# Expert layer of a hybrid transformer: all column groups of the whole float32 passes held together in one order, last piece first

## The chip, the cores and the metric

The kernel runs on one core of a Trainium2 chip. The metric is the device time of one execution in microseconds (us); the lower the better. Times of before are the median of three runs; the profile is of one further execution.

## What is computed

Two layers of a backbone over 256 latent and 256 context tokens of width 1024. Layer 0 ends in a dense SwiGLU, layer 1 in a mixture of eight SwiGLU experts, each token going to the two with the highest logits. The change is in the experts alone:

```python
def swiglu(h, w_gu, w_down):
    g, u = jnp.split(h @ w_gu, 2, axis=-1)
    return (jax.nn.silu(g) * u) @ w_down

def moe_swiglu(h, w_router, w_gu, w_down):
    logits = (h @ w_router).astype(jnp.float32)
    top_v, top_i = lax.top_k(logits, TOP_K)
    gates = jax.nn.softmax(top_v, axis=-1)
    out = jnp.zeros_like(h)
    for e in range(N_EXPERTS):
        w_e = jnp.sum(jnp.where(top_i == e, gates, 0.0), axis=-1).astype(h.dtype)
        out = out + w_e[..., None] * swiglu(h, w_gu[e], w_down[e])
    return out
```

All is float32; an expert has a hidden width of 1408, so its weights are 11.5 MB of gate-and-up and 5.8 MB of down.

## The kernel before

Everything up to the experts (the two mixers and the dense feed-forward) takes the first 840 us or so and is not touched.

The experts are sorted by the number of their tokens. Tokens are gathered into slots, 128 to a pass, and the slots of a pass are the rows of the output in PSUM, one slot to a partition. `PASSES` says which experts a pass holds: four passes have 128 slots of one expert; one has 32 slots of expert 1 and 96 of expert 4; one has 64, 32 and 32 slots of experts 5, 6 and 7. `Piece` (line 233 on) is the part of a pass that belongs to one expert. A pass of one expert is *split*: its weights come from HBM into a raw buffer, ScalarE rounds them to `wh` (line 268), VectorE takes the rest `wl` (line 271), and TensorE does three fast matmuls of 128x512 for each product. There are three pairs of `wh` and `wl`. A pass of several experts is *whole*: its pieces use the raw float32 weights without splitting, and each matmul handles a quarter of 32 slots, that is 32 columns of the TensorE array and 32 partitions of PSUM. A quarter is a **column group**: group 0 writes partitions 0 to 31, group 1 partitions 32 to 63, and so on. `product` (line 1523) issues them; a piece of 64 slots gives two matmuls, of 96 three.

`expert` (line 1474) is one job: 22 blocks of gate-and-up weights per expert (six column tiles `nt`, of two or four blocks `b`; a block holds two steps `kk` of the contraction, in the last `nt` four of half width), then 11 of down weights `f`. `blocks` (line 1503) loads a block of each expert of the job, in the order of the pieces; `products` (line 1532) is called for each `kk` and issues the matmuls of all pieces of a pass:

```python
            for c in pieces:
                self.mgu = product(out, c, get(c), ws[c.expert], s, start, stop)[-1]
```

`moe` (line 1632) runs the four jobs of `JOBS` in turn. The third job has a split pass (expert 1) and the whole pass of experts 1 and 4 (tiles `xgv` and `aTv`). Beside them runs the job called `last`, the whole pass of experts 5, 6 and 7 (tiles `xgw` and `aTw`): it is a generator, advanced at the steps that the table `LAST` names, so that its gate-and-up lies among the other jobs' work, and its down passes (per half `h` of the output) end the program.

Instructions are put in order by a scheduler that simulates the program, engine by engine, from the order of writing and the data they need; `inorder` (line 516) adds a dependence without a semaphore, so that one instruction stands behind another on its engine. Before, the pieces of a whole pass write different partitions and read different weights, and nothing holds their matmuls together.

Loads are issued by SP's queue in a fixed order into a ring of buffers: five of the pool `rawp`, eight of the pool `act`, one or two slots in old activations (`raw`, line 274). A load waits until the last reader of its buffer is done. SP also reads the number of experts with too many tokens (`overi`, line 1850), for the branch at the end.

Of the kernel before, what the change touches and what calls it, by code (L numbers as in the profile page):

```python
# [239 lines left out]
class Kern:  # L240
# [1233 lines left out]
    def expert(self, eids, passes, ys, last=False):  # L1474
# [28 lines left out]
        def blocks(gu, *at):  # L1503
            ws = {}
            for e in eids:
                if gu and self.w0:
                    ws[e] = None, self.w0.pop(0)
                    continue
                nt, b = at
                if gu:  # L1510
                    ap = a["mg0"][self.eid[e], nt, b] if nt < 5 else a["mg1"][self.eid[e], b]
                    n, parts = 1024, 1
                elif last:
                    n = min(2, 11 - nt)
                    ap = a["md"][self.eid[e], nt:nt + n, :, b * 512:b * 512 + 512].rearrange("f p c -> p f c")
                    n, parts = n * 512, n
                else:
                    ap, n, parts = a["md"][self.eid[e], nt], 1024, 1
                r = self.raw(ap, n, parts, split=e not in whole)
                ws[e] = r, self.split(r) if e in split else None  # L1520
            return ws

        def product(out, c, x, w, s, start, stop):
            if c.whole:
                return [self.mm(out[c.row + q:c.row + q + QUART], x[:, 0, q:q + QUART], w[0][:, s], start=start, stop=stop)
                        for q in range(0, c.n, QUART)]
            wh, wl = (t[:, s] for t in w[1])
            return [self.mm(out, x[:, 0], wh, start=start, stop=False),
                    self.mm(out, x[:, 0], wl, start=False, stop=False),
                    self.mm(out, x[:, 1], wh, start=False, stop=stop)]  # L1530

        def products(out, pieces, get, ws, s, start, stop):

            for c in pieces:
                self.mgu = product(out, c, get(c), ws[c.expert], s, start, stop)[-1]

        for nt in range(6):
            hw = 256 if nt < 5 else P
            kb = 2 if nt < 5 else 4
            ps = [self.ps("g", "mgu") for _ in passes]  # L1540
            for b in range(8 // kb):
                ws = blocks(True, nt, b)
                for p, (pieces, _) in zip(ps, passes):
                    for kk in range(kb):
                        k = b * kb + kk
                        products(p[:, :2 * hw], pieces, lambda c: c.x[:, :, k], ws,
                                 slice(kk * 2 * hw, kk * 2 * hw + 2 * hw), k == 0, k == 7)
                if (last or b % 2) and b < 8 // kb - 1:
                    yield
            for p, (pieces, _) in zip(ps, passes):  # L1550
                th = self.tmp("mth")[:, :hw]
                A.activation(th, p[:, :hw], AF.Tanh, scale=0.5)
                V.scalar_tensor_tensor(th, th, 1.0, p[:, :hw], op0=OP.add, op1=OP.mult)
                self.glu = V.scalar_tensor_tensor(th, th, 0.5, p[:, hw:2 * hw], op0=OP.mult, op1=OP.mult)
                trans(pieces, th, nt, hw // P)
            yield
# [10 lines left out]
        if last:  # L1567
            pieces, gate = passes[0]
            ys += [mp.tile([P, 2, 512], F32R, tag="ymoe", name="ylast", bufs=2),
                   mp.tile([P, 512], F32, tag="aT", name="ylast1", bufs=1)]  # L1570
            for h in range(2):
                p = self.ps("g", "mdn")
                for f in range(11):
                    if f % 2 == 0:
                        ws = blocks(False, f, h)
                    products(p, pieces, lambda c: c.a[:, :, f], ws, slice(f % 2 * 512, f % 2 * 512 + 512), f == 0, f == 10)
                    if f % 2:
                        yield
                for q in range(2):
                    s = slice(q * 256, q * 256 + 256)  # L1580
                    y = self.tmp("yg")[:, :256] if h == 0 else ys[1][:, s]
                    self.ylast = V.scalar_tensor_tensor(y, p[:, s], gate(), self.rowg[:, 2 * h + q],
                                                        op0=OP.mult, op1=OP.mult)
                    if h == 0:
                        self.hilo(ys[0], s, y)
                yield
            return
        py = [[self.ps("g", "mdn") for h in range(2)] for _ in passes]
        for f in range(11):
            ws = blocks(False, f, 0)  # L1590
            for pys, (pieces, _) in zip(py, passes):
                for h in range(2):
                    products(pys[h], pieces, lambda c: c.a[:, :, f], ws, slice(h * 512, h * 512 + 512), f == 0, f == 10)
            if f % 2:
                yield
# [292 lines left out]
```

## Time and profile before

| | before |
|---|---|
| median of 3 runs | 1285.9 us (1285.56 to 1288.61) |
| profiled execution | 1285.85 us |
| its span, first to last instruction | 1284.1 us |
| TensorE (PE) busy | 1248.9 us, 97% |
| VectorE (DVE) busy | 693.7 us, 54% |
| ScalarE (ACT) busy | 498.9 us, 39% |
| DMA | 263.12 MB, mean 205 GB/s |

The profile's page gives busy times over the whole span, and then groups of instructions. Further views answer questions about a stretch: busy time by window, the instructions of an engine in order of time, who waited for whom, and the chain of work that ended last. PE is the matmul, PEld the load of its stationary operand, which overlaps. In the views a tile is named as out<-in; `mgu` is a gate-and-up result in PSUM, `mdn` a down result. A matmul's recorded length contains its way through the pipe, so how long it occupies TensorE is read from the start of the next.

### The profile page before, as it was taken

The page shows a single profiled execution, that of the slowest core. Times are in us where ns is not written, and L with a number is a line of the kernel's source. Part 1 is how long each engine was busy: PE and PEld are TensorE (multiplying, and loading weights), DVE is VectorE, ACT ScalarE, POOL GpSimd, SP SyncE. Part 2 cuts the span into 40 slices and gives each one's busy share as a digit, 9 for nine tenths or more (in the row PEclk, how much of TensorE's full clock was granted, in tenths as well). Part 3 has the DMA queues.
Part 4 walks back from the last instruction along what each step waited for, and adds up shares of the span by engine and source line. Part 5 has one row for each costly group of instructions (what it writes and reads, how often), then busy time and mean ns, then how long its engine had stood idle before and what let it go on. Part 6 is the DMA issues. An engine that isn't in the chain of part 4 may idle for free.

```text
span 1284.1 us, 18115 instructions
## 1 busy us (share of the span) xinstructions
PE 1248.9 (97%) x6654; PEld 866.6 (67%) x6654; DVE 693.7 (54%) x1523; ACT 498.9 (39%) x938; POOL 8.9 (1%) x30
## 2 busy tenths in 40 slices
PE   6999999999999999999999999989999999999995
PEld 3777666777878888888868878955656533545632
DVE  4554674356433443443367777677767533446741
ACT  3443543224322322322235445545655323444521
POOL 0000000000000000000000000000000000000000
PEclk9999999999999999999999999999999999999998
DMA  9535343539342223222224553569897887699695
GB/s 379 203 132 197 131 141 122 176 135 390 106 157 89 92 99 99 91 89 99 99 75 141 194 212 130 188 227 372 317 372 289 308 287 295 218 368 353 249 368 208
DMA packets 82849, 263.12 MB, mean 205 GB/s; under 512 B 8128, under 2 KB 16448, under 8 KB 82752
## 3 DMA queue, kind: packets, MB, share of 16 engines
q1 hardware_dynamic: 82176, 259.79, 55.6%
q0 software_dynamic: 576, 2.10, 0.5%
q8 instruction: 54, 0.88, 0.3%
q14 instruction: 43, 0.35, 0.1%
HBM read 260.80 MB, written 1.05 MB: 204 GB/s over the span
## 4 chain that ended last, share of the span: by engine, by line
PE 91%; DMA 4%; DVE 2%; ACT 2%; issue 1%; SPq 0%; ACTq 0%; DVEq 0%
PE g L326 21%; PE mgu L326 18%; PE dps L326 10%; PE gps L326 9%; PE ups L326 9%; PE mdn L326 8%; PE adaps L326 4%; DMA raw<-in_md_dram 3%; PE vps L326 2%; PE attS L326 2%; PE rowbc L326 1%; PE yps L326 1%; PE scat L326 1%; PE gath L326 1%; PE attO L326 1%
## 5 line engine op out<-in xcount | busy, mean ns | idle before, releaser
L271 DVE TENSOR_TENSOR wl<-raw,wh 128x512 fp32r<-128x512 f32 (+1 forms) x354 | 300.6, 878 | 209.9 <-ACT wh L268 208.3
L268 ACT ACTIVATE wh<-raw 128x512 fp32r<-128x512 f32 (+1 forms) x354 | 262.3, 780 | 310.7 <-PE dps L326 80.8
L326 PE MATMUL g<-hmix,wh 128*128 128x512 f32 (+1 forms) x640 | 182.6, 364 | 0.3 <-DVE hmix L537 0.2
L326 PEld LDWEIGHTS g<-hmix,wh 128*128 128x128 f32 x640 | 112.6, 189 | 33.7 <-issue 11.0
L326 PE MATMUL gps<-hffn,wh 128*128 128x512 f32 x320 | 125.6, 395 | 0.0
L326 PE MATMUL ups<-hffn,wh 128*128 128x512 f32 x320 | 125.5, 394 | 0.0
L326 PE MATMUL mgu<-wh,xg 128*128 128x512 f32 (+1 forms) x384 | 120.9, 384 | 1.0 <-ACT wh L268 1.0
L326 PE MATMUL g<-hmix,wl 128*128 128x512 f32 (+1 forms) x320 | 115.5, 361 | 0.0
L326 PE MATMUL dps<-aT,wh 128*128 128x512 f32 x352 | 111.1, 394 | 0.0
L326 PEld LDWEIGHTS mgu<-wh,xg 128*128 128x128 f32 x384 | 70.2, 188 | 30.9 <-ACT wh L268 10.3
L326 PEld LDWEIGHTS dps<-aT,wh 128*128 128x128 f32 x352 | 66.0, 188 | 16.6 <-ACT wh L268 0.8
L326 PE MATMUL mgu<-wl,xg 128*128 128x512 f32 (+1 forms) x192 | 76.5, 398 | 0.4 <-DVE wl L271 0.2
L326 PE MATMUL mgu<-raw,xgw 128*32 128x512 f32 (+1 forms) x376 | 72.0, 564 | 0.3 <-DMA raw<-in_mg_dram 0.3
L326 PEld LDWEIGHTS gps<-hffn,wh 128*128 128x128 f32 x320 | 60.4, 189 | 14.9 <-DVE gth L1120 0.8
L326 PEld LDWEIGHTS ups<-hffn,wh 128*128 128x128 f32 x320 | 60.5, 189 | 14.2
L326 PE MATMUL dps<-aT,wl 128*128 128x512 f32 x176 | 69.6, 396 | 0.0
L326 PEld LDWEIGHTS g<-hmix,wl 128*128 128x128 f32 x320 | 60.4, 189 | 8.4 <-issue 0.9
L326 PE MATMUL ups<-hffn,wl 128*128 128x512 f32 x160 | 63.4, 396 | 0.0
L326 PE MATMUL gps<-hffn,wl 128*128 128x512 f32 x160 | 63.4, 396 | 0.0
L326 PE MATMUL mgu<-raw,xgv 128*32 128x512 f32 (+1 forms) x384 | 61.8, 563 | 0.0
L326 PE MATMUL mdn<-wh,aT 128*128 128x512 f32 x176 | 59.7, 404 | 0.0
L326 PEld LDWEIGHTS mgu<-wl,xg 128*128 128x128 f32 x192 | 36.1, 188 | 33.2 <-DVE wl L271 12.6
(356 smaller groups left out, 1725.7 us busy)
## 6 DMA issues: line engine op xcount, KB each, us to landing
raw<-in_mg_dram SPq DMA_DIRECT2D x162, 512.0 KB, 6.4
raw<-in_ada_dram SPq DMA_DIRECT2D x96, 512.0 KB, 5.0
raw<-in_md_dram SPq DMA_DIRECT2D x79, 512.0 KB, 7.4
raw<-in_fg_dram SPq DMA_DIRECT2D x44, 512.0 KB, 3.5
raw<-in_wi_dram SPq DMA_DIRECT2D x40, 512.0 KB, 4.9
raw<-in_fd_dram SPq DMA_DIRECT2D x22, 512.0 KB, 3.2
raw<-in_wo_dram SPq DMA_DIRECT2D x16, 512.0 KB, 5.0
xres<-in_mg_dram SPq DMA_DIRECT2D x9, 512.0 KB, 6.3
```

The source lines that it names most:

```text
L268: up = self.A.activation(h, src, AF.Copy)
L271: sub = self.V.tensor_tensor(lo, src, h.bitcast(F32), op=OP.subtract)
L326: return self.E.matmul(out, l, r, start=start, stop=stop, skip_group_check=True)
```

## The change

`products` now takes the pieces in reverse, so that the piece whose weights are loaded last goes first, and for a whole pass it holds all matmuls of one call in that order, behind the last matmul of the call before on the same block. A split pass has one piece and is as it was.

```diff
         def products(out, pieces, get, ws, s, start, stop):
 
-            for c in pieces:
-                self.mgu = product(out, c, get(c), ws[c.expert], s, start, stop)[-1]
+
+            ms = [m for c in reversed(pieces) for m in product(out, c, get(c), ws[c.expert], s, start, stop)]
+            if pieces[0].whole:
+                self.inorder(ws.setdefault("turn", [])[-1:] + ms)
+                ws["turn"] = ms
+            self.mgu = ms[-1]
```

What the scheduler makes of it on TensorE, in the second job, where one block of the job `last` lies among the split matmuls of the gate-and-up (`raw,xgw` are whole matmuls, `wh,xg` and `wl,xg` split ones). Before:

```order
3081 L326 MATMUL mgu<-raw,xgw 32x512 x2
3082 L326 MATMUL mgu<-wl,xg 128x512
3083 L326 MATMUL mgu<-wh,xg 128x512 x2
3084 L326 MATMUL mgu<-raw,xgw 32x512
3085 L326 MATMUL mgu<-wl,xg 128x512
3086 L326 MATMUL mgu<-wh,xg 128x512
3087 L326 MATMUL mgu<-raw,xgw 32x512 x5
3088 L326 MATMUL mgu<-wh,xg 128x512
```

Now:

```order
3070 L326 MATMUL mgu<-wl,xg 128x512
3071 L326 MATMUL mgu<-wh,xg 128x512 x2
3072 L326 MATMUL mgu<-raw,xgw 32x512 x8
3073 L326 MATMUL mgu<-wl,xg 128x512
3074 L326 MATMUL mgu<-wh,xg 128x512 x2
```

The eight whole matmuls of the block stand together where the last five stood.

On TensorE in the third job's gate-and-up, `raw,xgv` being the whole pass of experts 1 and 4. Before:

```order
3285 L326 MATMUL mgu<-raw,xgv 32x512
3286 L326 MATMUL mgu<-wh,xg 128x512
3287 L1494 MATMUL atr<-constp,mth 128x128 x2
3288 L326 MATMUL mgu<-raw,xgv 32x512 x7
3289 L326 MATMUL mgu<-wl,xg 128x512
```

Now:

```order
3260 L326 MATMUL mgu<-wh,xg 128x512 x2
3261 L1494 MATMUL atr<-constp,mth 128x128 x2
3262 L326 MATMUL mgu<-raw,xgv 32x512 x8
3263 L326 MATMUL mgu<-wl,xg 128x512
3264 L326 MATMUL mgu<-wh,xg 128x512 x2
```

The one matmul of expert 1 that stood ahead has joined the seven.

On TensorE at the end, where the down passes of `last` begin among those of the fourth job. Before:

```order
3681 L326 MATMUL mdn<-raw,aTw 32x512
3682 L326 MATMUL mdn<-wl,aT 128x512
3683 L326 MATMUL mdn<-wh,aT 128x512 x2
3684 L326 MATMUL mdn<-wl,aT 128x512
3685 L326 MATMUL mdn<-wh,aT 128x512
3686 L326 MATMUL mdn<-raw,aTw 32x512 x5
```

Now:

```order
3630 L326 MATMUL mdn<-raw,aTw 32x512 x8
3631 L326 MATMUL mdn<-wl,aT 128x512
3632 L326 MATMUL mdn<-wh,aT 128x512
3633 L326 MATMUL mdn<-wl,aT 128x512
3634 L326 MATMUL mdn<-wh,aT 128x512
3635 L326 MATMUL scat<-selT,ymoe 128x256 x2
3636 L326 MATMUL mdn<-raw,aTw 32x512 x8
```

Here too a block of 2, 1 and 5 has become one run of 8. The order of loads on SP is the same but for a few neighbours in the first two jobs, and the read of `overi`, which moves ahead of eight loads.

## Rows read from the trace of the kernel before

**Rows 1.** Busy time by stage: window, length, PE, PEld, DVE, ACT, POOL (instructions), PE clock, DMA share, GB/s

```profile
844.00:1004.00 160.00, 157.54 (x764) 98.58 (x763) 114.48 (x289) 90.19 (x188) 0.00 (x0) 1.00 0.90 336
1004.00:1114.00 110.00, 109.71 (x686) 46.26 (x684) 46.70 (x97) 36.12 (x81) 0.00 (x0) 1.00 0.76 276
1114.00:1153.00 39.00, 39.00 (x251) 16.65 (x248) 16.34 (x28) 15.05 (x28) 0.00 (x0) 1.00 0.91 333
1153.00:1223.50 70.50, 70.16 (x388) 43.73 (x387) 52.33 (x103) 39.16 (x79) 0.00 (x0) 1.00 0.82 298
1223.50:1270.00 46.50, 45.06 (x250) 17.17 (x250) 10.30 (x22) 5.70 (x12) 0.00 (x0) 1.00 0.96 355
```

**Rows 2.** Matmuls in order of time, third job: start us, length us, engine, line, tiles, shape, count

```profile
1018.12 0.64 PE L326 MATMUL mgu<-wh,xg 128*128 128x512 f32 x2
1018.59 0.40 PE L326 MATMUL mgu<-wl,xg 128*128 128x512 f32 x1
...
1019.15 1.05 PE L326 MATMUL mgu<-raw,xgv 128*32 128x512 f32 x2
1020.13 0.50 PE L326 MATMUL mgu<-wh,xg 128*128 128x512 f32 x1
...
1026.08 1.06 PE L326 MATMUL mgu<-raw,xgv 128*32 128x512 f32 x8
1027.08 0.50 PE L326 MATMUL mgu<-wl,xg 128*128 128x512 f32 x1
...
1027.73 1.06 PE L326 MATMUL mgu<-raw,xgv 128*32 128x512 f32 x8
```

**Rows 3.** Matmuls in order of time, one block of the job `last` in the second job

```profile
923.97 1.05 PE L326 MATMUL mgu<-raw,xgw 128*32 128x512 f32 x4
...
925.83 1.05 PE L326 MATMUL mgu<-raw,xgw 128*32 128x512 f32 x2
...
927.46 1.91 PE L326 MATMUL mgu<-raw,xgw 128*32 128x512 f32 x10
929.30 0.50 PE L326 MATMUL mgu<-wh,xg 128*128 128x512 f32 x1
```

**Rows 4.** Matmuls in order of time, whole matmuls of half width, third job

```profile
1107.99 1.07 PE L326 MATMUL mgu<-raw,xgv 128*32 128x256 f32 x16
1109.00 0.44 PE L1494 MATMUL atr<-constp,mth 128*128 128x128 f32 x2
```

**Rows 5.** Matmuls in order of time, first block of `last`; in brackets idle time and releaser

```profile
851.66 1.05 PE L326 MATMUL mgu<-raw,xgw 128*32 128x512 f32 x4 [0.35 <-DMA raw<-in_mg_dram]
852.90 1.04 PE L326 MATMUL mgu<-rawo,xgw 128*32 128x512 f32 x2 [0.20 <-DMA rawo<-in_mg_dram]
...
855.84 0.62 PE L326 MATMUL mgu<-rawo,xgw 128*32 128x512 f32 x1 [0.53 <-DMA rawo<-in_mg_dram]
855.85 0.62 PE L326 MATMUL mgu<-raw,xgw 128*32 128x512 f32 x2
```

**Rows 6.** Who waited for whom, 844 to 1284: us in total, times, longest

```profile
PEld mdn L326 <- DMA raw<-in_md_dram: 7.7, 10, 1.2
PEld mgu L326 <- DMA raw<-in_mg_dram: 5.8, 16, 0.8
```

**Rows 7.** Waits of SP's queue, which issues the loads, 844 to 1284

```profile
SPq L307 <- PE mgu L326: 131.1, 70, 7.3
```

**Rows 8.** Busy time by window in the first job, columns as in the first group

```profile
857.60:870.40 12.80, 12.80 (x54) 8.41 (x53) 10.34 (x20) 9.25 (x19) 0.00 (x0) 1.00 1.03 412
...
857.60:902.00 44.40, 44.40 (x221) 28.45 (x221) 34.62 (x105) 26.16 (x55) 0.00 (x0) 1.00 1.00 381
```

**Rows 9.** DMA queues, 1219.3 to 1270: packets, MB, share of 16 engines; then the issues

```profile
q1 hardware_dynamic: 9024, 17.30, 93.5%
...
raw<-in_md_dram SPq DMA_DIRECT2D x30, 512.0 KB, 10.2
raw<-in_md_dram SPq DMA_DIRECT2D x6, 256.0 KB, 9.2
```

**Rows 10.** Chain of work that ended last, 1215 to 1284: start us, us, what

```profile
1219.32 4.16 DMA raw<-in_md_dram
```

**Rows 11.** Instructions of line 1850, the read of the overflow count: count, ns, first and last start us

```profile
L1850 SPq TENSOR_LOAD <-overi x1: 292/292/292, 914.8 to 914.8; - x1
```

## The prediction

> **What bounds the kernel now.** I read busy time by stage first, then the matmuls in order of time, then the waits, for the engines and for the queue that issues the loads. The profiled execution took 1285.85 us (span 1284.1 and 1.75 around it), which is the median of the runs (1285.9), so the sum below is made against 1285.85. The change touches only the experts, from about 844 us on, and I cut that part into five: A, the first two expert jobs (844 to 1004); B, the gate-and-up passes of the third job (1004 to 1114); C, its down passes (1114 to 1153); D, the fourth job (1153 to 1223.5); E, the down passes of the job called "last" (1223.5 to 1270). In A to D TensorE is busy for 376.4 of 379.5 us at a granted clock of 1.00 (the 2.4 GHz level), with VectorE at 42 to 74% and DMA at 0.76 to 0.91 of its time [rows 1]. What TensorE does there is therefore on the path, unless something else is close behind it.
>
> A busy TensorE is not a well-used one, and the order of time shows it. A whole float32 matmul writes 32 of the 128 output partitions, and the trace has two records for each. A run with one such matmul (x2) lasts 0.98 us until the next matmul starts (1019.15 to 1020.13); a run of four on different column groups (x8) lasts 1.00 (1026.08 to 1027.08) [rows 2]. Four cost what one costs. A run of five (x10, from 927.46) lasts 1.84 [rows 3]. I call a **slot** what runs side by side: matmuls that follow each other on different column groups, until a group comes again. From one slot to two the run grows: a slot costs 0.86 us (1.84 less 0.98) however full it is, and half of that at half width (16 records, two half slots, 1.01 us in all) [rows 4].
>
> A run also costs something to enter and leave. From 1026.08 to 1027.73 one slot and two ordinary matmuls take 1.65 us; ordinary ones follow each other at 0.235 (two from 1018.12 to 1018.59) [rows 2]. 1.65 - 0.86 - 0.47 = 0.32 us per run.
>
> **The change, step by step.** It removes and adds no instruction of a kind: same matmuls, same loads. It puts pieces together.
>
> For the "last" job's gate-and-up (pieces of 64, 32 and 32 slots, so column groups 0 and 1, then 2, then 3), a block of two k stands before as runs of 2, 1 and 5: groups 01, then 2, then 3012 and 3, four slots in three runs; after, 8 in one run, two slots. In the trace these are the x4, x2 and x10 records at 923.97, 925.83 and 927.46 [rows 3]. For the third job's mixed pass (pieces of 32 and 96), 1 and 7 become 8: three slots and two runs become two and one. I counted the whole order in this way, before against after:
> - A: 41 slots in 30 runs, now 22 in 11. 19 x 0.86 + 19 x 0.32 = 22.4 us. In the very first block TensorE waited for the third expert's weights anyway, until 855.84 [rows 5]; two slots and a run stood ahead of that moment and their removal only lengthens the wait, 2.0 us. Left: 20.4.
> - B: 65 slots and 8 half ones in 36 runs, now 51 and 9 in 27. 13.5 x 0.86 + 9 x 0.32 = 14.5.
> - C: nothing (22 slots in 12 runs both times: there the two pieces already stood together).
> - D: 13 slots and 11 halves in 16 runs, now 11 and 8 in 9. 3.5 x 0.86 + 7 x 0.32 = 5.2.
> - E: 28 slots in 13 runs, now 22 in 7: 7.1 us of TensorE, which I cost at nothing. What hides it is the loader: 36 loads, 17.30 MB, take 0.94 of all DMA time from the issue of the first to 1270 [rows 9]: they land in an unbroken stream, and TensorE has nothing to do with how fast. If that cover were thin the 7.1 us would come in addition; if the held order keeps a slot back until the third weights are there, up to one slot, 0.9 us, would be lost.
>
> Sum on TensorE ahead of E: 20.4 + 14.5 + 5.2 = 40.1 us.
>
> E begins when its first load is issued, at 1219.32 [rows 10], and that load waits for a buffer that the fourth job's splitting frees. The splitting follows TensorE through its three buffers of split weights, so E moves up with D.
>
> Now what is close behind. **VectorE**: in 857.6 to 902 it is busy 34.62 of 44.40 us [rows 8]. Three blocks of the last job lie in it; each loses two slots and two runs, 2.4 us, so the stretch would shrink to 37.2 and VectorE would stand at 93%, with only three buffers of split weights between it and TensorE. I charge half of the 7.2 us there. **DMA**: loads reach 412 GB/s when the queue is full (857.6 to 870.4) [rows 8]. A moves 336 GB/s x 160 us = 53.8 MB, 130 us at that rate: 30 us of room for 20.4. B and D have 36 and 19 us of room for 14.5 and 5.2. So the loader follows on the whole, though not in each stretch; I charge 1 us. In SP's queue a few loads of A change places with a neighbour, which costs nothing as long as they come early. The read of the overflow count, at 914.8 before [rows 11], now stands ahead of eight loads that it stood behind; SP may wait there for VectorE to make the count, by at most what those eight loads take (8 x 512 KB at 381 GB/s, 11 us) and more likely by a few us, with some fifteen buffers loaded or loading by then. I cost it at nothing, and at 11 us for the range.
>
> The added order: between pieces it makes TensorE wait for the piece whose weights come last. What stands behind it in TensorE's queue is all the ordinary work, and VectorE and ScalarE wait for that. It costs nothing while the third weights are there in time. All waits of TensorE for expert weights from 844 on are 5.8 + 7.7 us [rows 6], while the loader waits 131.1 us for buffers that TensorE has yet to read [rows 7]: loads wait for TensorE, not TensorE for loads. From both sides: nothing as now, or at most two landings of 512 KB at 412 GB/s, 2.5 us, per block if the loads had no lead. I take nothing, since both rows stand on that side.
>
> 40.1 - 3.6 - 1 = 35.5. **Forecast: 1285.85 - 35.5 = 1250 us.**
>
> The row says that four groups cost what one costs. The Trainium skill, "TensorE: Matmul & The Clock Gate", Part 3, Measured speedup, gives less for packing: 2.38 for three column tiles and 3.07 for four row tiles, so that a full group would cost 1.3 of a single matmul. With a pair at the price of one, the slots ahead of E would by that give back some 25 us instead of 29, and the forecast would be some 1254; the trace differs (1.00 against 0.98 us) and I go by it.
>
> **Rivals.**
> 1. The loader or VectorE takes back much of it. For: in 857.6 to 902 DMA already moves 381 GB/s, and D has 0.82 with an idle stretch at its end, so it is fuller before. If the gain is lost wherever these two are near their limit, that is all 7.2 us of 857.6 to 902, about as much for the three blocks of the second job near 950 to 980 where loads come fast, and half of D: 17 us less than 40.1, so 23 us, 1263. Against: the 131 us that the loader stands waiting. Chance 0.18.
> 2. It gets **slower**: the order turns the last weights into a wait. Place: each of the 22 blocks of the "last" job's gate-and-up. Price: before, groups 0 and 1 could start on the first weights; now all wait for the third, two landings or 2.5 us later, 55 us over 22 blocks. It decides where the loads' lead over TensorE is under 2.5 us, as in the first block [rows 5]. If the lead were gone everywhere: 1285.85 + 55 - 40.1 = 1301. Against it stand the two waits [rows 6, 7]. Chance 0.03.
> 3. It does not do what it says: column groups that read different weights do not run side by side, so that the slots stay. Then only the runs count, 34 of them ahead of E x 0.32 = 11 us, 1275. Against: at 855.84 two different weight buffers start within 0.02 us [rows 5]. Chance 0.03.
> 4. Nothing to be seen, within 0.3% (3.9 us, about what a measurement of this kernel can tell): a reshuffle of the order elsewhere (the gather of tokens moves by some matmuls) eats all. The stages run at 99% TensorE, so there is little slack for it to upset. Chance 0.02.
>
> **Numbers.** The forecast has 0.74. Its own range is 1241 (nothing charged for VectorE and DMA, and some of E) to 1257. The range that should hold 8 in 10 reaches into rival 1: 1240 to 1268. Faster by over 0.3%: 0.74 + 0.18 + 0.03 = 0.95. Same: 0.02. Slower: 0.03.
>
> **What would show it.** Right: in the trace after, runs of the last job read x16 and last about 1.85 us, none is x2; A shrinks to some 140 us, B to 96, C stays at 39, D at about 65; E stays near 47 from its first load to its last; TensorE's waits for expert weights stay under some 20 us and DMA rises above 0.95 in A. VectorE in the first job goes above 0.85. Wrong: an x16 run that lasts over 2.1 us (slots are not free), waits for the mg loads of tens of us (rival 2), or stage C longer.

## The result, and the profile after

| | before | after |
|---|---|---|
| median (lowest to highest, 4 runs each, side by side) | 1286.3 us (1285.56 to 1288.61) | **1246.88 us** (1245.71 to 1248.32) |
| profiled execution; span | 1285.85; 1284.1 | 1245.71; 1243.9 |
| TensorE busy | 1248.9 us, 97% | 1198.1 us, 96% |

The ratio of after to before is 0.9691, 95% interval 0.9674 to 0.9709: 39.4 us less, where 1250 us was forecast and 1240 to 1268 given as the range.

The view by stage, with the cuts moved to where the stages now begin (busy time of each engine, granted clock, DMA share, GB/s), answers to [rows 1] in the same columns:

```profile
844.00:984.30 140.30, 136.88 (x771) 98.90 (x770) 115.21 (x292) 90.48 (x188) 0.00 (x0) 0.98 0.99 383
984.30:1081.40 97.10, 97.10 (x690) 45.96 (x689) 47.37 (x99) 36.82 (x83) 0.00 (x0) 1.00 0.86 321
1081.40:1121.40 40.00, 40.00 (x254) 17.49 (x252) 17.93 (x29) 16.32 (x31) 0.00 (x0) 1.00 0.89 334
1121.40:1185.80 64.40, 63.84 (x382) 42.85 (x381) 51.28 (x101) 37.06 (x75) 0.00 (x0) 1.00 0.87 325
1185.80:1230.00 44.20, 33.29 (x242) 13.34 (x243) 8.79 (x20) 5.68 (x12) 0.00 (x0) 1.00 0.95 351
```

A, B, C and D last 140.3, 97.1, 40.0 and 64.4 us; the prediction named 140, 96, 39 and 65. In A DMA has gone to 0.99 of its time. In A the clock is 0.98 and TensorE is idle for 3.4 us: that was not foreseen, and one place holds most of both (below). VectorE in the first job was to go above 0.85 and stands at 0.84.

What the change was to make, a block of the last job in one run, stands in the order of time of TensorE in the first job:

```profile
869.62 0.61 PE L326 MATMUL mgu<-wh,xg 128*128 128x512 f32 x2
870.16 1.93 PE L326 MATMUL mgu<-raw,xgw 128*32 128x512 f32 x16
872.01 0.50 PE L326 MATMUL mgu<-wl,xg 128*128 128x512 f32 x1
```

16 records, that is eight whole matmuls, last 1.85 us until the next starts (870.16 to 872.01). Before, five of them lasted 1.84 and the first three had runs of their own [rows 3]. All blocks of the last job in A and B stand like this. In D the first three are still cut, into 10 and 6, 6 and 10, and 14 and 2 records, so that the sign "none is x2" did not quite come true; the prediction's count of D, 11 slots and 8 halves in 9 runs, has these cuts in it.

The first block of the last job is the exception. In order of time, and then in windows across it:

```profile
853.09 0.40 PE L326 MATMUL mgu<-wl,xg 128*128 128x512 f32 x1
856.54 1.07 PE L326 MATMUL mgu<-rawo,xgw 128*32 128x512 f32 x2 [3.06 <-DMA rawo<-in_mg_dram]
...
857.40 1.06 PE L326 MATMUL mgu<-rawo,xgw 128*32 128x512 f32 x2
...
859.83 0.50 PE L326 MATMUL mgu<-wl,xg 128*128 128x512 f32 x1
```

```profile
849.70:853.10 3.40, 3.40 (x21) 2.91 (x19) 2.62 (x9) 1.90 (x5) 0.00 (x0) 1.00 0.87 306
853.10:856.50 3.40, 0.39 (x2) 0.00 (x0) 2.04 (x10) 0.37 (x1) 0.00 (x0) 0.94 0.95 353
856.50:859.90 3.40, 3.36 (x17) 0.66 (x17) 0.00 (x0) 0.00 (x0) 0.00 (x0) 0.56 1.02 416
859.90:863.30 3.40, 3.40 (x15) 2.81 (x16) 1.99 (x4) 2.65 (x6) 0.00 (x0) 1.00 1.02 414
```

TensorE waits 3.06 us for the third expert's weights, and then works at a granted clock of 0.56: a pass over all four groups takes 0.86 us (856.54 to 857.40) where half of the 0.86 us of a slot is usual, so the clock stands at the lower of its two levels, 1.2 GHz. The block takes 3.29 us instead of 1.85.

For E, the DMA queue from the issue of its first load (1178.7) to 1229.4, and the loads in the chain that ended last. These answer to [rows 9, 10]:

```profile
q1 hardware_dynamic: 9024, 17.30, 93.3%
...
raw<-in_md_dram SPq DMA_DIRECT2D x30, 512.0 KB, 10.7
raw<-in_md_dram SPq DMA_DIRECT2D x6, 256.0 KB, 9.3
```

```profile
1183.53 11.85 DMA raw<-in_md_dram
...
1195.51 9.36 DMA raw<-in_md_dram
...
1204.99 10.02 DMA raw<-in_md_dram
...
1215.12 10.71 DMA raw<-in_md_dram
```

The same 36 loads with the same 17.30 MB, now from 1178.7 on instead of 1219.3, take 0.93 of all DMA time, and the chain that ended last is four loads one behind the other. E has moved up by 40.6 us and is no shorter for it: from the issue of the first load to the landing that the chain waits for last it takes 47.0 us before (1219.32 to 1266.33) and 47.1 now (1178.70 to 1225.83).

The waits of TensorE and its weight loads for expert weights, 844 to the end, against [rows 6]:

```profile
PEld mdn L326 <- DMA raw<-in_md_dram: 16.9, 13, 3.8
PE mdn L326 <- DMA raw<-in_md_dram: 9.8, 10, 2.9
PEld mgu L326 <- DMA rawo<-in_mg_dram: 3.5, 1, 3.5
PE mgu L326 <- DMA rawo<-in_mg_dram: 3.1, 1, 3.1
PEld mgu L326 <- DMA raw<-in_mg_dram: 2.7, 8, 0.4
```

Those for down weights (`md`) have grown. They lie in E, all but 0.7 us of the 16.9, where TensorE is through sooner and waits for the stream. By the weight loads alone the waits for expert weights are 16.9 + 3.5 + 2.7 = 23.1 us, so that the prediction's sign, under some 20 us, failed; it failed in E, where TensorE's time does not count (e2 below). Those for gate-and-up weights (`mg`) are the one wait of the first block and little else. In SP's queue the loader's wait for TensorE has shrunk by about the gain, from 131.1 [rows 7] to 92.0 us, and its wait for the overflow count is 0.6 us:

```profile
SPq L307 <- PE mgu L326: 92.0, 41, 6.3
...
SPq L1854 <- DVE overi L1362: 0.6, 1, 0.6
```

### The profile page after: what moved, and what is told of

Read it like the earlier page. It is cut to its first block, busy times and chain, and to the rows that moved or that the text cites. A ratio compares the mean times of both kernels' runs of the same rounds, so it can differ in the third digit from the quotient of the medians.

```text
span 1243.9 us, 18096 instructions
## 1 busy us (share of the span) xinstructions
PE 1198.1 (96%) x6654; PEld 862.0 (69%) x6654; DVE 692.7 (56%) x1523; ACT 498.6 (40%) x938; POOL 8.9 (1%) x30
## 4 chain that ended last, share of the span: by engine, by line
PE 90%; DMA 5%; DVE 2%; ACT 1%; issue 1%; SPq 1%; ACTq 0%; DVEq 0%
PE g L326 22%; PE mgu L326 17%; PE dps L326 10%; PE gps L326 9%; PE ups L326 9%; PE mdn L326 7%; PE adaps L326 3%; DMA raw<-in_md_dram 3%; PE vps L326 2%; PE attS L326 2%; PE rowbc L326 1%; PE yps L326 1%; PE gath L326 1%; PE attO L326 1%; PE scat L326 1%; PE attT L757 1%
## 5 line engine op out<-in xcount | busy, mean ns | idle before, releaser
L326 PE MATMUL mgu<-wh,xg 128*128 128x512 f32 (+1 forms) x384 | 117.5, 380 | 0.0
L326 PE MATMUL adaps<-raw,s 128*32 128x512 f32 x384 | 56.6, 619 | 0.2 <-DMA raw<-in_ada_dram 0.2
L1099 DVE SCALAR_TENSOR_TENSOR xres<-dps,mods,xres 128x256 f32<-128x256 f32 x64 | 27.6, 478 | 43.3 <-PE dps L326 43.3
```

The source lines that it names most:

```text
L326: return self.E.matmul(out, l, r, start=start, stop=stop, skip_group_check=True)
L1099: self.V.scalar_tensor_tensor(self.x[:, d, s], ps[:, s], gt[:, j:j + 1], self.x[:, d, s], op0=OP.mult, op1=OP.add)
```

## The experiments

In all of them a "unit" is 0.86 us, what one full-width whole matmul occupies its column group for. Stage lengths in the table are of the profiled executions, in us, from the start of TensorE's first matmul of each stage; the last column is the end of TensorE's last matmul. A begins with the first split expert matmul, B with the first of `xgv`, C with the first of `aTv`.

| kernel | median | ratio to before (95%) | A begins | A | B | C, D, E | ends |
|---|---|---|---|---|---|---|---|
| before | 1286.3 | 1 | 844.98 | 159.59 | 112.16 | 155.20 | 1271.93 |
| after | 1246.88 | 0.9691 (0.9674 to 0.9709) | 845.99 | 138.33 | 97.11 | 150.09 | 1231.53 |
| e1 reversed, not held | 1245.14 | 0.9683 (0.9670 to 0.9696) | 847.52 | 136.58 | 97.02 | 149.82 | 1230.94 |
| e2 E as before | 1244.83 | 0.9677 (0.9664 to 0.9690) | 847.85 | 136.58 | 97.02 | 149.56 | 1231.00 |
| e3 last job's gate-and-up only | 1258.68 | 0.9792 (0.9777 to 0.9807) | 844.70 | 136.33 | 112.25 | 149.62 | 1242.90 |
| e4 group after group | 1258.25 | 0.9783 (0.9768 to 0.9798) | 845.32 | 138.68 | 102.96 | 156.10 | 1243.06 |
| e5 two by two | 1247.26 | 0.9682 (0.9665 to 0.9699) | 845.37 | 136.45 | 97.60 | 153.97 | 1233.39 |
| e6 third job only | 1272.82 | 0.9887 (0.9867 to 0.9908) | 845.27 | 159.34 | 97.11 | 156.56 | 1258.29 |
| e7 first block later | 1244.55 | 0.9667 (0.9651 to 0.9682) | 845.36 | 135.81 | 97.13 | 151.61 | 1229.92 |
| e8 two down steps earlier | 1239.98 | 0.9628 (0.9612 to 0.9644) | 847.53 | 137.41 | 97.11 | 147.17 | 1229.22 |
| e9 first blocks at 5 and 7 | 1238.77 | 0.9623 (0.9610 to 0.9637) | 846.40 | 134.82 | 97.08 | 146.72 | 1225.03 |
| e10 three down steps earlier | 1256.33 | 0.9757 (0.9743 to 0.9772) | 845.67 | 135.90 | 97.13 | 161.32 | 1240.02 |
| e11 three steps, only in D | 1237.18 | 0.9609 (0.9592 to 0.9627) | 846.24 | 134.85 | 97.09 | 143.90 | 1222.08 |

The start of A scatters by 3 us over these profiles, before anything that they touch; so stages are compared by length. One thing still makes the lengths of A unequal: in e1, e2, e3, e5, e6, e7 and e10 the first 2.0 to 2.6 us of A lie at the lower clock, in e4 1.0 us, in the others none. In e1 it is

```profile
847.50:849.70 2.20, 2.20 (x11) 1.91 (x10) 1.76 (x9) 0.73 (x2) 0.00 (x0) 0.50 0.09 32
```

Differences of 1 us between the A of two runs are therefore not read as an effect of the edit.

**e1: is it the reversal or the holding?**

```diff
...
             ms = [m for c in reversed(pieces) for m in product(out, c, get(c), ws[c.expert], s, start, stop)]
-            if pieces[0].whole:
-                self.inorder(ws.setdefault("turn", [])[-1:] + ms)
-                ws["turn"] = ms
             self.mgu = ms[-1]
```

> Only the reversal of the pieces; the added dependences are left out. Theory (the reversal alone does it: the built program has the same instructions in the same order on every engine as the changed kernel): 1247 us, ratio 0.969, as the change. Rival (holding does it, the reversal nothing): 1286 us. Since the programs are equal, this run also says how well the change's time repeats.

Measured: 1245.14 us, ratio 0.9683; the interval overlaps that of the change. The reversal does all of it. The counterpart, pieces forward and held, was not run: its program has the instructions of before in the order of before, on every engine. So the added dependences change nothing, in either order. I read the order before and now in this way, which no run tests by itself: written forward, a piece whose weights come early is ready early and the scheduler sends it ahead alone; written in reverse, the first piece in the order of writing is the last to be ready, and when it is, so are the others.

This profile also shows the first block without the slow clock: the wait was 1.59 us there, and the passes follow each other at 0.43 to 0.45 us.

```profile
857.62 0.62 PE L326 MATMUL mgu<-rawo,xgw 128*32 128x512 f32 x2 [1.59 <-DMA rawo<-in_mg_dram]
...
858.07 0.60 PE L326 MATMUL mgu<-rawo,xgw 128*32 128x512 f32 x2
```

**e2: does TensorE's time count in E?** `products` issues the down passes of the last job by the loop of before; the rest is the change. `down` is a new argument of `products`, true in the call for these passes alone.

```diff
+            if not (not down):
+                for c in pieces:
+                    self.mgu = product(out, c, get(c), ws[c.expert], s, start, stop)[-1]
+                return
```

> The change as it is, but the down passes of the last job (stage E) are issued as before: 28 slots in 13 runs there again instead of 22 in 7, 7.1 us more of TensorE by the prices 0.86 and 0.32 us. Theory (E is set by its loads): within 1.5 us of the change, 1247 us, and the stream of its loads stays at 49 us from the first issue to the last landing. Rival (the change's 1.8 us beyond the predicted 35.5 + 2.8... came from E, so TensorE counts there): 1252 to 1254 us.

Measured: 1244.83 us, beside 1245.14 of e1 on the same chip. C, D and E together last 149.56 us against 149.82. The 6 slots and 6 runs in E are worth nothing; E is set by its loads. The two profiles say it a second time: in e1's TensorE had a clock of 0.51 from 1208.1 to 1215.0, in E, in e2's 1.00, and this did not lengthen e1's either.

**e3 and e6: the two halves.** The loop of before stays for all but the last job's gate-and-up (e3, below), or for all of the last job (e6, with the condition `not (not last)`).

```diff
+            if not (last and not down):
+                for c in pieces:
+                    self.mgu = product(out, c, get(c), ws[c.expert], s, start, stop)[-1]
+                return
```

> Reversed and held only in the gate-and-up of the last job (pieces of 64, 32 and 32); the third job's whole pass and the down passes of the last as before. Counts: A 22 slots in 11 runs (as the change), B 69 and 8 half slots in 36 runs (before 65 and 8 in 36, the change 51 and 9 in 27), D 11 and 8 half in 10. Theory of slots and runs: B costs 3.4 us more than before (four slots more, since now the two jobs' runs meet on the same column group), that is 18 us more than in the change; the sum 1247 + 17.9 + 0.3 = 1265 us, stage B about 115 us, A 138. Rival (only the number of runs counts, the 40 us being 1.18 us for each of the 34 runs): 25 runs fewer than before, 1286 - 29.5 = 1256.5 us, and B stays at 112.

> The complement of e3: reversed and held only in the third job's whole pass; all of the last job as before. Counts against before: A equal, B 55.5 slots for 69 and 27 runs for 36, D 19.5 slots for 18.5 and 16 runs. Theory of slots and runs: B 14.5 us less (97 to 98 us), D 0.9 more, the rest as before, 1286 - 13.6 = 1272 us. Rival (the gain is that of the whole stream, not of a place, so that the loader or VectorE takes back a part alone): not 1272 but 1278 or more. With e3 the two parts should add up: e3 and this together save what the change saves, within 2 us.

Measured: e3 1258.68 us (by the theory 1265, by the rival 1256.5), e6 1272.82 (1272, or 1278 and more). Each stage moved where its own part was changed: A 159.6 to 136.3 in e3 and not in e6, B 112.2 to 97.1 in e6 and not in e3; C, D and E together 155.2 to 149.6 in e3 and to 156.6 in e6, where D was expected to grow by 0.9. The savings of the two add up, 2.08% + 1.13% = 3.21%, to that of the change (3.09% here, 3.17% in e1). In e3 the rule of slots failed in one point: B should have grown by four slots, 3.4 us, and stayed as it was (112.25). The rival fits the 112 and the median, but e6 has B 15 us shorter with only nine runs fewer, 1.7 us for each, where the rival has 1.18 for all. Both counts were off; e4 shows how.

**e4: one group after the other.** In the whole gate-and-up passes the matmuls of a block are written group by group, all `kk` of one group before the next.

```diff
...
+                               for c in reversed(pieces) for q in range(0, c.n, QUART) for kk in range(kb)]
+                        self.inorder(ms)
...
```

> As the change, but within a block of the whole gate-and-up passes the matmuls are issued column group after column group (all steps of the contraction of one group, then the next group) instead of all groups for one step. Same matmuls, same runs (11, 27, 9 in A, B, D), but more slots: A 55 for 22, B 123 and 26 half for 51 and 9, D 22 and 26 half for 11 and 8. Theory of slots (only matmuls that follow each other on different column groups go side by side): 133.5 slots x 0.86 = 115 us more, 1362 us; a block of 16 records lasts about 4.4 us instead of 1.85. Rival (what counts is that the run is not interrupted): 1247 us, 1.85 us.

Measured: 1258.25 us, 13 more than e1 and neither 115 nor nothing. In order of time, a full-width block and then, in the half-width column tile, runs of eleven, five and fifteen matmuls (22, 10 and 30 records), and a half-width block of sixteen in D:

```profile
869.55 1.94 PE L326 MATMUL mgu<-raw,xgw 128*32 128x512 f32 x16
871.43 0.50 PE L326 MATMUL mgu<-wl,xg 128*128 128x512 f32 x1
...
1071.80 3.27 PE L326 MATMUL mgu<-raw,xgv 128*32 128x256 f32 x22
1075.00 0.44 PE L1494 MATMUL atr<-constp,mth 128*128 128x128 f32 x2
1075.37 1.92 PE L326 MATMUL mgu<-raw,xgv 128*32 128x256 f32 x10
1077.22 0.39 PE L326 MATMUL mgu<-wh,xg 128*128 128x256 f32 x1
...
1079.75 4.16 PE L326 MATMUL mgu<-raw,xgv 128*32 128x256 f32 x30
1083.84 0.50 PE L326 MATMUL mdn<-wh,aT 128*128 128x512 f32 x1
...
1172.21 4.59 PE L326 MATMUL mgu<-raw,xgw 128*32 128x256 f32 x32
1176.74 0.33 PE L1494 MATMUL atr<-constp,mth 128*128 128x128 f32 x1
```

The full block takes 1.88 us, as in the change (1.85), though only neighbouring matmuls at the borders of groups differ in group: five slots by the prediction's rule. So matmuls need not alternate. The first block shows what happens. In the program, TensorE has there

```order
2918 L326 MATMUL mgu<-rawo,xgw 32x512 x4
2919 L326 MATMUL mgu<-raw,xgw 32x512 x4
```

and on the chip they start as

```profile
855.71 0.63 PE L326 MATMUL mgu<-rawo,xgw 128*32 128x512 f32 x2 [2.43 <-DMA rawo<-in_mg_dram]
855.74 0.63 PE L326 MATMUL mgu<-raw,xgw 128*32 128x512 f32 x2
856.17 0.68 PE L326 MATMUL mgu<-rawo,xgw 128*32 128x512 f32 x2
856.20 0.71 PE L326 MATMUL mgu<-raw,xgw 128*32 128x512 f32 x2
```

A `raw` matmul, fifth to be issued, starts 0.03 us after the first and ahead of the second pass of `rawo`. Each group works off its own matmuls. How many may wait in a group, the half-width runs tell. If one runs and one more can wait behind it, so that a third for the same group stops the issue for all groups, the three runs need 7, 4 and 9 half units (groups 1111 2222 333, then 3 0000, then 111 2222 3333 0000), and a block of 16 needs 10. Measured are 3.20, 1.85 and 4.09 us, and 4.53 for the block of 16 in D: 0.447 us for each half unit more, on one line (1.85 + 3 x 0.447 = 3.19, + 5 x 0.447 = 4.09, + 6 x 0.447 = 4.53). With two waiting the counts are 5, 4, 6 and 7, which is not that line. With none waiting they are 9, 4, 12 and 13, which is not that line either, and the full block of 1.88 us would need five units.

Now e3's B comes out too: counted by the fullest group of each run it needs 69 units, as many as before. And e4's own 13 us: 5 units more in B and 9 in D are 12.0 us. Measured are 5.9 us in B and 6.3 in C, D and E, 12.2 in all against e1. By stage it is not as counted; the third job's first whole down run, with which C begins, is of 16 records in e4 and cut into 8 and 8 in e1, so that the border between B and C lies at another point of the work.

**e5: a test of that reading.** As e4, but with two `kk` per group and turn.

```diff
...
+                               for k0 in range(0, kb, 2) for c, q in gs for kk in (k0, k0 + 1)]
```

> As e4_group_after_group, but in the half-width blocks (four steps of the contraction) each column group takes two steps in turn instead of four; in the full-width blocks two steps per group, as there. New theory from e4, where a run of 16 records lasted 1.85 us in that order too: each column group works off its own matmuls, one running and one waiting behind it, and a run lasts 0.86 us for each matmul of its fullest group; TensorE stalls only where a third one for the same group comes. By that the half-width blocks lose their stall: against the change only 3 units of 0.86 us more, in D, where runs are cut differently; 1248 to 1250 us, and e4's half-width runs of 4.16 us are gone. Rival (the prediction's slots: only matmuls that follow each other on different groups go side by side): 55, 132 and 31 slots in A, B and D, about 108 us more, 1355 us. Rival (e4's 12 us came from its order as such, in full-width blocks too): 1258 us again.

Measured: 1247.26 us, ratio 0.9682, that of the change; the 2.6 us expected for three units more in D do not show in it. The last half-width run of the third job, thirteen matmuls, is down to 4 half units:

```profile
1075.39 1.95 PE L326 MATMUL mgu<-raw,xgv 128*32 128x256 f32 x26
1077.27 0.50 PE L326 MATMUL mdn<-wh,aT 128*128 128x512 f32 x1
```

By the prediction's rule it would be seven. Order inside a run is free, as long as no group gets a third matmul while its first still runs.

**e7: the first block later.**

```diff
-LAST = (2, 5, 8, 10, ...
+LAST = (3, 5, 8, 10, ...
```

> As the change, but the first block of the last job is put one step of the first job later (first entry of LAST 3 instead of 2). In the change TensorE waits 1.3 to 3.1 us for that block's third weights, and in two of four profiles with this order the granted clock then fell to 0.5 to 0.6 for some 4 us. Theory: the wait goes, and with it the slow stretch: 1242 to 1244 us, stage A 134.5 to 136 us, clock 1.00 throughout 850 to 865. Rival (the loader sets that place: DMA is at 0.99 of its time in A, so the wait only moves to the next block or to a split one): 1245 to 1247 us, A 136.5 to 138.5.

Measured: 1244.55 us; the interval overlaps those of the change and e1. The wait is 1.03 us, not gone, at a clock of 1.00; A is 135.8. Inconclusive: one step is too little to tell. (Where the expectation counts two profiles of four with a slow stretch, it was two of five: after and e4, of after and e1 to e4.)

**e8: two of E's twelve down steps earlier.**

```diff
-LAST = (2, 5, 8, 10, 13, 16, 18, 21, 24, 27, 29, 32, 34, 36, 38, 41, 48, 50, 52, 55, 58, 60)
+LAST = (3, 5, 8, 10, 13, 16, 18, 21, 24, 27, 29, 32, 34, 36, 38, 41, 46, 48, 50, 52, 54, 56, 60, 62)
...
         for i in range(12):
-            next(last)
+            if i >= len(LAST) - 22:
+                next(last)
```

> As e7, and the last job's remaining gate-up blocks come a little earlier (LAST ends 46, 48, 50, 52, 54, 56 instead of 48, 50, 52, 55, 58, 60), so that the first two of its twelve down steps can lie beside the fourth job's down passes (steps 60 and 62). Six loads of 512 KB (3.1 MB, 8 us of E's stream of 49) are issued earlier, where DMA is at 0.87 of its time in D. Theory (E is set by its stream of loads alone): E ends 8 us after less of a stream, D takes 4.1 us more of TensorE, net 4 us less than e7: 1238 to 1241 us. Rival (the loads in D take the place of others and E's stream only starts as much later as it is shorter, or the buffers do not come free earlier): as e7, 1242 to 1246 us.

Measured: 1239.98 us; the ratio is 0.4% below e7's, 5 us for an expected 4, and the intervals don't overlap. C, D and E together went from 151.61 to 147.17, and the fourth job's DMA share from 0.87 (e7, 1118.0 to 1182.5) to 1.00 (e8, 1122 to 1177). The earlier gate-and-up blocks, which made room for the two down steps, were not run alone. That E is bound by its stream is therefore not only a reason why a gain was lost there: filling DMA time that D left over gets it back. This profile had a wait of 2.14 us at the first block and the slow clock again (0.59 from 857.1):

```profile
855.00:857.10 2.10, 0.02 (x1) 0.00 (x0) 1.67 (x9) 0.37 (x1) 0.00 (x0) 1.00 0.98 388
857.10:860.00 2.90, 2.84 (x16) 0.56 (x16) 0.00 (x1) 0.00 (x0) 0.00 (x0) 0.59 1.02 412
```

**e9: and the first blocks at steps 5 and 7.** Against e8:

```diff
-LAST = (3, 5, 8, 10, 13, ...
+LAST = (5, 7, 9, 11, 13, ...
```

> As e8, but LAST starts 5, 7, 9, 11 instead of 3, 5, 8, 10, so that the split blocks of the first job get their weights first and the last job's first block comes two steps later. Theory (the wait of 1.0 to 3.1 us at the first block is that of a loader which has nothing ahead there, and later it has): no wait for its weights, no slow stretch, stage A 1.5 to 3 us shorter than e8's 137.4: 1237 to 1239 us. Rival (the wait moves to the split blocks, as it did for one step in e7): TensorE waits about as long for other mg loads before 865, A stays at 136 to 137.5, 1239 to 1241 us.

Measured: 1238.77 us. The wait for the first block's weights and the slow clock are gone (clock 0.99 and 1.00 from 846 to 870), A is 134.8, 2.6 less than e8's. In the medians the step is 1.2 us, inside the intervals, so that the gain itself is not shown.

**e10: three down steps earlier.** Against e8:

```diff
-... 38, 41, 46, 48, 50, 52, 54, 56, 60, 62)
+... 38, 41, 43, 46, 48, 50, 52, 54, 60, 61, 62)
```

> As e8, but three of the twelve down steps lie beside the fourth job's (LAST ends 43, 46, 48, 50, 52, 54, 60, 61, 62), and one gate-up block of the last job has moved into the third job's down passes, where e8 has DMA at 0.77 of its time. Three loads more (4 us of stream) leave E. Theory (stream-bound end): a further 1.5 to 3 us, 1237 to 1239 us. Rival (DMA is at 1.00 in e8's fourth job, 1122 to 1177, so more loads there only delay the fourth job's own): 1240 to 1243 us, with waits of TensorE for md loads in D.

Measured: 1256.33 us, a miss on both sides. C has become longer: from its first matmul to the fourth job's first split one it lasts 54.0 us, where it is 38.9 in e8. D and E together are not longer (107.3 us, 108.2 in e8). C shows it in a window and in TensorE's order of time:

```profile
1081.40:1121.40 40.00, 35.65 (x199) 12.50 (x191) 10.25 (x16) 9.45 (x18) 0.00 (x0) 0.96 0.59 217
```

```profile
1088.51 1.91 PE L326 MATMUL mdn<-raw,aTv 128*32 128x512 f32 x12
...
1091.02 1.05 PE L326 MATMUL mdn<-raw,aTv 128*32 128x512 f32 x4
...
1113.68 1.32 PE L326 MATMUL mdn<-wh,aT 128*128 128x512 f32 x2 [4.35 <-ACT wh L268]
```

DMA falls to 0.59 there (0.84 in the same window of e9), TensorE waits there once for 4.35 us, and five of the third job's whole down runs, in the change ten of 16 records and two of 8, are broken, three of them into 12 and 4.

**e11: three down steps, but none of the last job's blocks in C.** Against e9:

```diff
-... 38, 41, 46, 48, 50, 52, 54, 56, 60, 62)
+... 38, 41, 46, 48, 50, 52, 54, 56, 60, 61, 62)
```

> As e9, with a third down step of the last job beside the fourth job's (LAST ends 60, 61, 62 instead of 60, 62); unlike e10, no gate-up block of the last job lies in the third job's down passes. It tells apart the two explanations of e10's 16 us over e8. Theory (the block of the last job in stage C did it: its loads and the third job's down loads hold each other's buffers, DMA falls to 0.58 in 1082 to 1122, the whole down runs break up): 1237 to 1240 us here, C 40 us long with 12 runs. Rival (the third down step did it): 1250 us or more.

Measured: 1237.18 us. So the third step does no harm; the gate-and-up block among the third job's down passes did. Nor is a gain of the third step shown: the interval overlaps e9's. That the two jobs' loads hold each other's buffers there was not shown by itself. **e11 beats both kernels**: 3.9% below before, 0.8% below the change, with intervals that don't overlap (0.9592 to 0.9627, 0.9674 to 0.9709).

## Why the prediction was right

**The prices** held in the main: a full group costs what one matmul costs. In A the 19 slots and 19 runs (22.4 us) came back as 23.0 (e1) and 23.3 (e3), in B 14.5 as 15.1. With the slots at 0.86 that leaves (23.0 - 16.3) / 19 = 0.35 and (15.1 - 11.6) / 9 = 0.39 us per run, where 0.32 was taken. The A of e1 is not quite comparable with that of before, though: its first 2.2 us lie at half the clock, which is worth 1.1, and its first block waits 1.59 us where before waits 0.35 + 0.20 + 0.53 [rows 5], 0.5 more. In the change's profile, where A is 21.3 us shorter, that wait is 2.0 longer than before and the slow block costs 1.4. Without these, A would have lost 24.6 us in e1 and 24.7 in the change, an estimate, and a run in A would cost some 0.44. So 0.32 was too small; the two prices were not measured apart. C, D and E together gave 5.4 (e1) for the 5.2 of D. C is unchanged, as said. The Trainium skill, "TensorE: Matmul & The Clock Gate", Part 3, Measured speedup, by which the forecast would have been some 1254 (an estimate), is again on the low side. Here the run of eight lasts 1.85 us, as long as a run of five did before, in two slots too (1.84), and the median is 1246.88.

**E at nothing** was right, as e2 shows; what shows in its place is the stream of loads, of equal length before and after. The overflow count at nothing was right, too (0.6 us).

**The charge of 3.6 us for VectorE and 1 us for DMA** was the mis-sized step. The three blocks of the first job that lie in it, each first and last cut at nearly the same work, in before and after:

```profile
855.80:900.00 44.20, 44.16 (x214) 26.83 (x214) 33.57 (x101) 25.51 (x53) 0.00 (x0) 1.00 1.00 382
```

```profile
856.50:895.00 38.50, 38.46 (x219) 26.42 (x220) 32.33 (x107) 24.67 (x53) 0.00 (x0) 0.96 1.02 408
```

It shrank by 5.7 us, although it holds the slow first block, which cost 1.4 (3.29 instead of 1.85): about all of the 7.2 us came back. VectorE stands at 0.84, not 0.93, and TensorE is busy for all but 0.04 us. The loader did reach its limit there (1.02, 408 GB/s) but it was still ahead: in 856.5 to 895 it waits 7.8 us for TensorE (12.2 before, in 857.6 to 902). Most of its 92 us lie elsewhere, 60.3 in B.

**The first block** was charged with 2.0 us, as slots whose loss only lengthens a wait. The wait is real, 1.0 to 3.1 us in the profiles of this order, and in the change's it grew by 2.0 us, as charged. What the prediction did not have is that the clock can fall behind that wait, 1.4 us more; the run price that was too small made up for it. Wait and clock make A 138.3 us in the change's profile and 136.6 in e1's, of the same program: in e1 the wait is 1.5 us shorter and the block 1.4, and the slow start takes back 1.1.

**The rule of slots** was right in price and wrong in wording: matmuls need not follow each other on different groups (e4, e5). It gave the right number because here the order of before and after runs round the groups, where both rules count alike; in e3 they part. **"The held order"** as the cause, in rival 2 and in the reading of the change, was wrong as well: the reversal alone does it (e1). The cost of rival 2 exists at the first block and hardly elsewhere (2.7 us in eight waits of weight loads). Rival 1 took nothing. Rival 3 is refuted by the run of 1.85 us, which reads three different weight buffers, rival 4 by the result.

The sum of 40.1 us is thus nearly what was measured, 39.4 between the medians and 40.1 between the profiled executions, and the forecast was 3 us too high by its reserve. That it agrees to a tenth with the profiled executions is luck in part: A, B and what follows are 21.3, 15.1 and 5.1 us shorter there, 41.4 together, and A began 1.0 us later; and in A the small run price and the slow clock offset each other.

## What to carry to other kernels

Where a scheduler fills an engine with whatever is ready, the order in which equal work is written can decide how it is grouped: try writing the part that becomes ready last first; here what was to stand together then did so without a fence. Count a packed run by its fullest column group, not by its matmuls, as long as no group is given a third matmul while its first runs, and look at what one record lasts until the next begins. And before counting a gain in the last stage, look whether its loads are an unbroken stream; if they are, the gain lies in starting them earlier (e8), not in the engine.

## What the runs showed of the hardware that was not expected

- Column groups take their matmuls out of the order of issue among each other: a matmul issued fifth started 0.03 us after the first (e4). The Trainium skill, "TensorE: Matmul & The Clock Gate", Part 3, The mechanism, has matmuls start and end strictly in the order of issue; these rows differ, and the rows decide. With one matmul running and one waiting in each group, four run lengths lie on one line of 0.447 us a half unit.
- The granted clock fell in the same place in some executions only. Behind waits of TensorE at the first block of 3.06 us (after), 2.43 (e4) and 2.14 (e8) it was 0.56, 0.70 and 0.59 in the next 2.4 to 3.4 us; behind waits of 1.59 (e1), 1.53 (e2), 1.26 (e3), 1.32 (e5 and e10) and 1.03 (e7) it stayed at 1.00. After and e1, one with and one without, are the same program; the block took 1.4 us more in the one with.
- The length of the wait alone does not decide it. The first line is from E of after, where the clock stays at 1.00 (1209.6 to 1213.0), the second from the fourth job of e11, where it is 0.64 (1169.3 to 1172.7), and 0.65 in the same place of e9:

```profile
1209.63 1.92 PE L326 MATMUL mdn<-raw,aTw 128*32 128x512 f32 x16 [2.90 <-DMA raw<-in_md_dram]
```

```profile
1169.33 0.50 PE L326 MATMUL mdn<-wl,aT 128*128 128x512 f32 x1 [1.69 <-DVE wl L271]
```
